# Attention of a hybrid encoder trunk: TensorE's order written out, products as a stream of steps between its parts, the sample keys in buffers of their own, the longest scores in a product's banks

## The chip, the cores and the metric

The kernel runs on one core of one Trainium2 chip. The core has a matrix engine (TensorE, PE in the profile, with its weight loads as PEld), a vector engine (VectorE, DVE), a scalar engine (ScalarE, ACT), a general engine (GpSimd, POOL) and SyncE (SP), which here issues transfers. Each engine works through its own queue of instructions in order; semaphores order the engines among each other. The metric is the device time of one execution in microseconds, the median of several runs; the profile comes from one execution, and its times have their zero at the start of that execution's span.

## The reference

The model is a trunk of two layers for 512 frames of one new stream (the prompt) and 8 running streams with 16 new frames each (the samples), 640 tokens in all, with 1024 features. What it computes, cut to what matters here:

```python
x += 0.5 * swiglu(rmsnorm(x, g1), w_gu1, w_down1)
h  = rmsnorm(x, gm)
z  = h @ w_in          # columns: conv B | conv C | conv V | q | k | v | gates
y_conv = B * causal_conv3(C * V)
# prompt: a frame reads its own chunk of 64 and the 8 before, 8 heads of 64
s = q @ k.T * 64 ** -0.5 + rel_bias[clipped distance]
y_attn = softmax(where(valid, s, -1e30)) @ v
# sample: 16 queries against 256 cached keys and their own 16
m = sigmoid(g_conv) * (y_conv @ w_conv_out) + sigmoid(g_attn) * (y_attn @ w_attn_out)
x += m @ w_o
x += 0.5 * swiglu(rmsnorm(x, g2), w_gu2, w_down2)
```

A final norm follows the layers. Outputs are the normed frames, the new keys and values, and the last two inputs of each convolution.

## The kernel before

The 640 tokens lie along the free axis, the features along the 128 partitions. All large products work in fp32 split in two parts: a weight tile of 128 × 128 is held as `whi` and `wlo`, an activation as `hhi` and `hlo` (with a suffix m for the mixer's norm), and a product sums hi·hi, hi·lo and lo·hi. `product` (L307 to L318) does this for one output tile: 8 weight tiles, three parts each, two halves of 320 tokens, 48 matmuls of 128x320 on L317. Its output `ps` is a tile of `acc`, PSUM's pool of two buffers with two banks each. The other PSUM pool, `att`, has four buffers with one bank each. Weights come in slabs of 512 KB: SP loads `raw` (L188), ACT rounds it to `whi` (L248), DVE takes the difference `wlo` (L253); there are three buffers of each.

A layer is a feed-forward part, the mixer and a second feed-forward part. The mixer norms x: `sums` (L400) adds the squares over the features with ten one-column matmuls (`npsm`), `roots` takes the root on ACT (L404) and the reciprocal on DVE (L405), `turn` (L410) spreads the result over a diagonal tile on DVE, and `nbcm` (L382) broadcasts it with matmuls into PSUM, from where ACT copies it to `rrm` (L383). The products do not wait for it: they take the unscaled x, and each result is scaled with `rrm` (`rr` in the code) on its way out of PSUM. The function `stats` that issues sums, root, turn and broadcast is called from within the first product of q, ahead of its sixth weight tile.

`attention` (L984) is the stage that the change touches. It projects q and k for each of the 4 pairs of heads (`qproj`, `kproj`: `pq`, `pk`), and v for all of them (`pv`, L1027). For each pair, `scores` issues for each block i of 128 queries the two heads' scores against the (i + 1) · 128 keys that a query of that block can see (`pss`, L1060; four blocks of 128 to 512 keys), and DVE adds the bias and takes the maximum while it reads them (L1062) into the tile `s`. `softmax` (L1188 to L1194) takes the exponent on ACT and normalises on DVE. `values` turns the weights (`ptp`, transposes on L1082, copied out by ACT and DVE on L1084), multiplies with v (`py`, L1095) and copies the result into `yas` (L1097). The samples follow: `sscores(b)` loads the cached keys and values of sample b (`kc` on L1126, `vc` on L1129, 512 KB each, and `vn` on L1132), copies the new keys behind the cached ones on POOL (L1133), computes the scores of all 8 heads (`spss`, L1136) and their softmax; `svalues(b)` transposes (`sptp`, L1151), copies out (`spt` on ACT, `spn` on DVE), multiplies with the values (`spy`, L1162), scales on ACT (`yx`, L1164) and transposes into the layout of `yas` (`ptx`, L1167).

`kc` and `vc` use the buffers of tag "s", two of them, which the prompt's weights `s` use as well. A new tile of that tag waits until the tile before the last has been read.

Beside the attention there are products that do not depend on it: the four channels of the convolution (`conv`: products `pc`, `pcv` and `pb`, each followed by DVE's work on the channel) and the first two gates (`pgate`). They are in the generator `others`, and each call of `other()` issues the next whole product. In `attention` no order is written out by hand: the scheduler of the compiler places each instruction in its engine's queue by its own estimate of when the operands are ready, so the code gives the data and a rough order only. The stage behind it (`outputs`) and the last product of the mixer have their order written (`manual_schedule`).

Of the kernel before, what the change touches and what calls it, by code (L numbers as in the profile page):

```python
# [138 lines left out]
def trunk(ctx: ExitStack, tc: tile.TileContext, xin, wst, small, pbias, samplebias, kcache, vcache,  # L139
# [167 lines left out]
    def product(ps, ops, at=()):  # L307
# [3 lines left out]
        for k, (xh, xl) in enumerate(ops):  # L311
# [3 lines left out]
            for j, (w, x) in enumerate(((wh, xh), (wh, xl), (wl, xh))):  # L315
                for a in range(2):
                    PE.matmul(ps[:, a, :HT], w, x[:, a * HT : (a + 1) * HT],  # L317
                              start=k == 0 and j == 0, stop=k == n - 1 and j == 2)  # L318

# [478 lines left out]
    def mixer(l, after):  # L798
        with tc.tile_pool(name=f"yp{l}", bufs=1, reuse_waits="tile") as yp:
# [5 lines left out]
            with tc.tile_pool(name=f"mp{l}", bufs=2, reuse_waits="tile") as mp:  # L805
# [3 lines left out]
                def gate(m, then=None):  # L809
                    pg = acc(f"pgate{l}_{m}")  # L810
                    product(pg, h)
# [10 lines left out]
                def others():  # L822
# [3 lines left out]
                    for m in range(2):  # L826
                        gate(m)
                        yield

                other = others()  # L830
                attention(l, h, st, stats, mp, yas, lambda: next(other, None))
# [152 lines left out]
    def attention(l, h, norms, stats, mp, yas, other):  # L984
# [11 lines left out]
        def qproj(p):  # L996
            pq = acc(f"pq{l}_{p}")
            product(pq, h, {5: stats} if p == 0 else {})
# [3 lines left out]
            for e in range(2):  # L1002
                r = slice(e * HD, (e + 1) * HD)
                POOL.tensor_copy(bd[r, :, p, e * TS : (e + 1) * TS],
                                 t[r, SEQ:].rearrange("p (b t) -> p b t", b=NB))

        def kproj(p):
            pk = acc(f"pk{l}_{p}")
            product(pk, h)
# [3 lines left out]
            POOL.tensor_copy(ks[:, p, :], t[:, SEQ:])  # L1013

        qproj(0)
        kproj(0)

# [26 lines left out]
        def scores(p):  # L1044
# [10 lines left out]
            for i in range(NQ):  # L1055
                w = (i + 1) * P
                pss = [att(f"pss{l}_{hh}_{i}")[:, :w] for hh in heads]
# [14 lines left out]
        def values(p):  # L1072
# [13 lines left out]
            for j in range(NQ):  # L1086
                for e in range(2):
                    turn(j, e)
                if j == 0:
# [9 lines left out]

        for p in range(npair):  # L1100
            scores(p)
            last = p == npair - 1
            if last:
                other()
                other()
            else:
                qproj(p + 1)
            vals = values(p)
            next(vals)
            if last:  # L1110
                other()
            else:
                kproj(p + 1)
# [8 lines left out]
        def sscores(b):  # L1122
            n = f"{l}_{b}"
            kc = mp.tile([P, offs[-1] + SEQ], F32, name=f"kc{n}", tag="s")
            kc = kc[:, : npair * KS].rearrange("p (a k) -> p a k", a=npair)
# [20 lines left out]
        def svalues(b):  # L1146
# [9 lines left out]
            DVE.tensor_copy(pn, ptp[:TS, 2 * P : 3 * P])  # L1156

# [6 lines left out]
            ACT.activation(yx, pys, AF.Copy, scale=st[:, 3, 0:1])  # L1164
            if b % G == 0:
# [10 lines left out]
        sscores(0)  # L1176
        for b in range(NB):
            if b + 1 < NB:
                sscores(b + 1)
            for _ in range(2 if b < 2 else 1):  # L1180
                other()
            svalues(b)
        other()
# [294 lines left out]
```

## Time and profile before

| | us |
|---|---|
| median of 3 runs | 2635.67 |
| lowest and highest | 2634.62, 2636.07 |
| the profiled execution | 2634.21 |
| its span in the profile | 2632.4 |
| TensorE busy | 2605.3 |
| DVE busy | 1832.0 |
| ACT busy | 1051.4 |
| POOL busy | 58.4 |

The span is what the profiler saw from the first to the last instruction; the execution's own time is 1.8 us longer. In rows of a timeline the first number is the start in microseconds from the span's start, the second the duration; then engine, line, operation, output and inputs by their names, shapes, and how often in a row; brackets at the end show the idle time of the engine before it and what released it. Matmuls overlap in a pipeline, so the pace is read from start to start and not from durations. In the view of waits a row has the total, the number of times and the longest in microseconds.

### The profile page before, as it was taken

To read this page: it belongs to the slowest core of one execution; us is meant where nothing else is said; L and a number is where in the kernel's file an instruction comes from. 1 tells how busy PE (TensorE), PEld (TensorE's weight loads), DVE (VectorE), ACT (ScalarE), POOL (GpSimd) and SP (SyncE) were. 2 spreads that over 40 slices of the span, in tenths; PEclk is the share of its full clock that TensorE was granted. 3 is DMA by queue.
4 is the path that set the end of the run, shared out by engine and by line. 5 is a ranking of instruction groups with operands and counts; after the bars stand their busy time and mean duration, and the time that the engine had idled before them with its cause. 6 is when DMAs were issued, how large, how long until landed. Compare 5 with 4: busy or idle time off the path is not lost.

```text
span 2632.4 us, 42588 instructions
## 1 busy us (share of the span) xinstructions
PE 2605.3 (99%) x17864; PEld 2544.0 (97%) x17864; DVE 1832.0 (70%) x2771; ACT 1051.4 (40%) x1586; POOL 58.4 (2%) x137
## 2 busy tenths in 40 slices
PE   8999999999999999999999999999999999999998
PEld 8999999888999999999999999998889999999998
DVE  7687676453677887767787677655546779867676
ACT  5343334332444543334453333334324445433333
POOL 0000000110000000000000000001010000000000
PEclk9999999999999999999999999999999999999999
DMA  3222222224122132222222222233241222222222
GB/s 130 77 100 81 79 91 99 104 97 140 69 93 81 65 106 88 73 89 81 81 81 96 88 82 73 89 103 112 96 146 57 89 81 73 97 89 81 80 92 78
DMA packets 73809, 237.07 MB, mean 90 GB/s; under 512 B 7984, under 2 KB 18864, under 8 KB 73616
## 3 DMA queue, kind: packets, MB, share of 16 engines
q1 hardware_dynamic: 70016, 223.90, 24.7%
q0 software_dynamic: 2880, 9.79, 1.0%
q8 instruction: 140, 2.29, 0.3%
q10 hardware_dynamic: 720, 0.65, 0.1%
q14 instruction: 53, 0.43, 0.1%
HBM read 225.85 MB, written 7.94 MB: 89 GB/s over the span
## 4 chain that ended last, share of the span: by engine, by line
PE 92%; DVE 4%; DMA 3%; ACT 1%; issue 1%; SPq 0%; DVEq 0%; ACTq 0%; POOLq 0%
PE pab L326 11%; PE pda L317 11%; PE pdb L317 11%; PE paa L326 10%; PE pcb L326 6%; PE pca L326 5%; PE py L317 4%; PE po L317 4%; PE qa L326 3%; PE pbb L326 3%; PE pba L326 3%; DMA kc<-in_kcache 2%; PE pq L317 2%; PE pgate L317 2%; PE pk L317 2%; PE pv L1027 2%
## 5 line engine op out<-in xcount | busy, mean ns | idle before, releaser
L253 DVE TENSOR_TENSOR wlo<-raw,whi 128x1024 fp32r<-128x1024 f32 (+2 forms) x492 | 530.7, 1083 | 162.5 <-ACT whi L248 162.4
L248 ACT CAST whi<-raw 128x1024 fp32r<-128x1024 f32 (+2 forms) x492 | 461.5, 941 | 395.3 <-PE pca L326 79.4
L326 PE MATMUL pab<-xhib,whi 128*128 128x320 f32 x704 | 218.4, 310 | 0.4 <-ACT u_b L721 0.4
L326 PE MATMUL pab<-xlob,whi 128*128 128x320 f32 x704 | 217.4, 309 | 0.0
L326 PE MATMUL pab<-xhib,wlo 128*128 128x320 f32 x704 | 217.4, 309 | 0.0
L326 PE MATMUL paa<-xhia,whi 128*128 128x320 f32 x640 | 198.2, 310 | 0.7 <-ACT c_a L657 0.5
L326 PE MATMUL paa<-xloa,whi 128*128 128x320 f32 x640 | 197.7, 309 | 0.0
L326 PE MATMUL paa<-xhia,wlo 128*128 128x320 f32 x640 | 197.7, 309 | 0.0
L317 PE MATMUL pda<-ahia,whi 128*128 128x320 f32 x704 | 160.4, 309 | 0.6 <-DVE x L787 0.6
L317 PE MATMUL pda<-aloa,whi 128*128 128x320 f32 x704 | 160.4, 309 | 0.0
L317 PE MATMUL pda<-ahia,wlo 128*128 128x320 f32 x704 | 160.4, 309 | 0.0
L317 PE MATMUL pdb<-alob,whi 128*128 128x320 f32 x656 | 149.6, 309 | 0.0
L317 PE MATMUL pdb<-ahib,whi 128*128 128x320 f32 x656 | 149.5, 309 | 0.0
L317 PE MATMUL pdb<-ahib,wlo 128*128 128x320 f32 x656 | 149.4, 309 | 0.0
L326 PEld LDWEIGHTS pab<-xhib,whi 128*128 128x128 f32 x704 | 132.2, 188 | 1.2 <-ACT u_b L721 0.9
L326 PEld LDWEIGHTS pab<-xlob,whi 128*128 128x128 f32 x704 | 132.2, 188 | 0.2
L326 PEld LDWEIGHTS pab<-xhib,wlo 128*128 128x128 f32 x704 | 132.2, 188 | 0.0
L326 PEld LDWEIGHTS paa<-xhia,whi 128*128 128x128 f32 x640 | 120.2, 188 | 1.3 <-ACT c_a L657 0.8
L326 PEld LDWEIGHTS paa<-xloa,whi 128*128 128x128 f32 x640 | 120.2, 188 | 0.1
L326 PEld LDWEIGHTS paa<-xhia,wlo 128*128 128x128 f32 x640 | 120.2, 188 | 0.0
L248 ACT CAST whi<-s 128x1024 fp32r<-128x1024 f32 (+1 forms) x96 | 94.2, 981 | 63.5 <-DVE s L192 52.0
L317 PEld LDWEIGHTS pda<-ahia,whi 128*128 128x128 f32 x704 | 117.6, 188 | 1.1 <-issue 1.1
(486 smaller groups left out, 6731.6 us busy)
## 6 DMA issues: line engine op xcount, KB each, us to landing
raw<-in_wst SPq DMA_DIRECT2D x384, 512.0 KB, 3.5
kc<-in_kcache SPq DMA_DIRECT2D x16, 512.0 KB, 4.3
vc<-in_vcache SPq DMA_DIRECT2D x16, 512.0 KB, 3.4
bias<-in_pbias POOLq DMA_DIRECT2D x16, 256.0 KB, 3.5
x<-in_xin SPq DMA_DIRECT2D x8, 320.0 KB, 5.4
out_ko<-k POOLq DMA_DIRECT2D x8, 320.0 KB, 2.4
out_vo<-v POOLq DMA_DIRECT2D x10, 256.0 KB, 3.0
out_yout<-x SPq DMA_DIRECT2D x8, 192.0 KB, 1.9
```

Source lines behind the costliest of these rows:

```text
L248: ACT.copy(hi[:, d], src[:, c])
L253: DVE.tensor_tensor(out=lo, in0=src, in1=hi.bitcast(F32), op=ALU.subtract)
L317: PE.matmul(ps[:, a, :HT], w, x[:, a * HT : (a + 1) * HT], start=k == 0 and j == 0, stop=k == n - 1 and j == 2)
L326: PE.matmul(ps, a, b, start=start and kp == 0 and j == 0, stop=stop and kp == NP - 1 and j == 2, skip_group_check=True)
L1027: PE.matmul(pv[t], xx[:, t * P : (t + 1) * P], w[:, kk * AW : (kk + 1) * AW], start=c == 0 and kk == 0 and j == 0, stop=c == KT // 2 - 1 a ...
```

## The change

`product` becomes the generator `steps`, which hands control back after each weight tile (6 matmuls); `product` itself runs it to the end. The products of q, k, the convolution and the gates are chained into one stream (`work`), and `fill(n)` issues the next n weight tiles of it. TensorE's order in `attention` is now the order in which the code issues: the stage stands under `manual_schedule` for that engine alone, the other engines keep the scheduler.

The order as written, in weight tiles: q_0 (with the norm's sums and broadcast, one directly behind the other, ahead of the sixth tile), k_0, v, 4 tiles; then for each pair the scores, 12 tiles, transposes of two key blocks, 2 tiles, transposes of the other two, 2 tiles, the weighted values. Then the scores of samples 0 and 1; for each sample 7 tiles (8 for odd ones), transposes, 2 tiles, values, the scores of the sample after the next, 2 tiles, the last transpose; at the end what is left of the stream.

The longest scores of the two heads of a pair (i = 3, 512 keys each) go to the two banks of one `acc` tile and are issued second. `kc` has its own tag, with two buffers.

```diff
--- before.py
+++ after.py
@@ -304,7 +304,7 @@
 
     tiles = Tiles()
 
-    def product(ps, ops, at=()):
+    def steps(ps, ops, at=()):
 
 
         n = len(ops)
@@ -316,6 +316,12 @@
                 for a in range(2):
                     PE.matmul(ps[:, a, :HT], w, x[:, a * HT : (a + 1) * HT],
                               start=k == 0 and j == 0, stop=k == n - 1 and j == 2)
+            if k < n - 1:
+                yield
+
+    def product(ps, ops, at=()):
+        for _ in steps(ps, ops, at):
+            pass
 
     def block(ps, s, half, ops, ks, start, stop):
 
@@ -807,8 +813,12 @@
                 gates = {}
 
                 def gate(m, then=None):
+                    for _ in gate_steps(m, then):
+                        pass
+
+                def gate_steps(m, then=None):
                     pg = acc(f"pgate{l}_{m}")
-                    product(pg, h)
+                    yield from steps(pg, h)
                     if then:
                         then()
                     gates[m] = tmp(f"g{l}_{m}")
@@ -824,11 +834,11 @@
                         yield from conv(l, c, h, rr, cn, ycs[c])
                     POOL.dma_start(co[l], cn)
                     for m in range(2):
-                        gate(m)
+                        yield from gate_steps(m)
                         yield
 
-                other = others()
-                attention(l, h, st, stats, mp, yas, lambda: next(other, None))
+                with tc.manual_schedule(engines={mybir.EngineType.PE}):
+                    attention(l, h, st, stats, mp, yas, others())
             with tc.tile_pool(name=f"gp{l}", bufs=1, reuse_waits="tile") as gp, \
                  tc.manual_schedule(engines=ORDERED):
                 hold[0] = True
@@ -981,7 +991,9 @@
         give(range(6, KT))
         return mo
 
-    def attention(l, h, norms, stats, mp, yas, other):
+    def attention(l, h, norms, stats, mp, yas, others):
+
+
         rr = norms.rr
         npair = H // 2
         nt = T // P
@@ -995,7 +1007,7 @@
 
         def qproj(p):
             pq = acc(f"pq{l}_{p}")
-            product(pq, h, {5: stats} if p == 0 else {})
+            yield from steps(pq, h, {5: stats} if p == 0 else {})
             t = qa[p] = mp.tile([P, T], F32, name=f"q{l}_{p}", tag="q")
             DVE.scalar_tensor_tensor(out=halves(t), in0=two(pq), scalar=HD ** -0.5,
                                      in1=halves(rr), op0=ALU.mult, op1=ALU.mult)
@@ -1003,17 +1015,32 @@
                 r = slice(e * HD, (e + 1) * HD)
                 POOL.tensor_copy(bd[r, :, p, e * TS : (e + 1) * TS],
                                  t[r, SEQ:].rearrange("p (b t) -> p b t", b=NB))
+            yield
 
         def kproj(p):
             pk = acc(f"pk{l}_{p}")
-            product(pk, h)
+            yield from steps(pk, h)
             t = ka[p] = mp.tile([P, T], F32, name=f"k{l}_{p}", tag="k")
             scaled(t, pk, rr)
             POOL.dma_start(ko[l, :, p, :], t)
             POOL.tensor_copy(ks[:, p, :], t[:, SEQ:])
-
-        qproj(0)
-        kproj(0)
+            yield
+
+        def work():
+            for p in range(1, npair):
+                yield from qproj(p)
+                yield from kproj(p)
+            yield from others
+
+        def fill(n):
+            for _ in range(n):
+                next(stream, None)
+
+        for _ in qproj(0):
+            pass
+        for _ in kproj(0):
+            pass
+        stream = work()
 
         rc = norms.r
         pv2 = [acc(f"pv{l}_{i}") for i in range(2)]
@@ -1052,9 +1079,14 @@
                 POOL.memset(bias[-1][0:CHUNK, SEQ - CHUNK :], NEG)
                 ss.append(mp.tile([P, offs[-1] + SEQ], F32, name=f"s{n}", tag="s"))
                 st.append(mp.tile([P, 4, NQ], F32, name=f"st{n}", tag="st"))
-            for i in range(NQ):
+
+            for i in (0, NQ - 1, *range(1, NQ - 1)):
                 w = (i + 1) * P
-                pss = [att(f"pss{l}_{hh}_{i}")[:, :w] for hh in heads]
+                if i == NQ - 1:
+                    both = acc(f"pss{l}_{p}")
+                    pss = [both[:, e, :w] for e in range(2)]
+                else:
+                    pss = [att(f"pss{l}_{hh}_{i}")[:, :w] for hh in heads]
                 for e in range(2):
                     r = slice(e * HD, (e + 1) * HD)
                     PE.matmul(pss[e], qa[p][r, i * P : (i + 1) * P], ka[p][r, :w], start=True, stop=True)
@@ -1086,7 +1118,7 @@
             for j in range(NQ):
                 for e in range(2):
                     turn(j, e)
-                if j == 0:
+                if j % 2:
                     yield
             py = att(f"py{l}_{p}")
             for j in range(NQ):
@@ -1097,20 +1129,15 @@
             ACT.copy(yas[:, p, 0:SEQ], py)
             yield
 
+        fill(4)
         for p in range(npair):
             scores(p)
-            last = p == npair - 1
-            if last:
-                other()
-                other()
-            else:
-                qproj(p + 1)
+            fill(12)
             vals = values(p)
             next(vals)
-            if last:
-                other()
-            else:
-                kproj(p + 1)
+            fill(2)
+            next(vals)
+            fill(2)
             next(vals)
 
 
@@ -1121,8 +1148,8 @@
 
         def sscores(b):
             n = f"{l}_{b}"
-            kc = mp.tile([P, offs[-1] + SEQ], F32, name=f"kc{n}", tag="s")
-            kc = kc[:, : npair * KS].rearrange("p (a k) -> p a k", a=npair)
+            kc = mp.tile([P, npair * KS], F32, name=f"kc{n}", tag="kc")
+            kc = kc.rearrange("p (a k) -> p a k", a=npair)
             SP.dma_start(kc[:, :, :PAST], kcache[l, b])
             vraw = mp.tile([P, offs[-1] + SEQ], F32, name=f"vc{n}", tag="s")
             vraw = vraw[:, : 2 * AW].rearrange("p (a k) -> p a k", a=2)
@@ -1154,6 +1181,7 @@
             pn = mp.tile([TS, P], F32, name=f"spn{n}", tag="spn")
             ACT.copy(pt, ptp[:, : 2 * P].rearrange("p (a b) -> p a b", a=2))
             DVE.tensor_copy(pn, ptp[:TS, 2 * P : 3 * P])
+            yield
 
             pys = att(f"spy{n}")[:, :P]
             for j, (w, v) in enumerate(((pn, vn), (pt[:, 0], vraw[:, 0]), (pt[:, 1], vraw[:, 1]))):
@@ -1162,6 +1190,7 @@
                     PE.matmul(pys[r], w[:, r], v[:, p * P : (p + 1) * P], start=j == 0, stop=j == 2)
             yx = mp.tile([P, P], F32, name=f"yx{n}", tag="yx")
             ACT.activation(yx, pys, AF.Copy, scale=st[:, 3, 0:1])
+            yield
             if b % G == 0:
                 ptx[0] = att(f"ptx{n}")
             PE.transpose(ptx[0][:, (b % G) * P : (b % G + 1) * P], yx, ident)
@@ -1174,13 +1203,18 @@
                         ptx[0][r].rearrange("p (b a e t) -> p a b e t", b=G, a=npair, e=2)[:, :, :, e, :])
 
         sscores(0)
+        sscores(1)
         for b in range(NB):
-            if b + 1 < NB:
-                sscores(b + 1)
-            for _ in range(2 if b < 2 else 1):
-                other()
-            svalues(b)
-        other()
+            vals = svalues(b)
+            fill(7 + b % 2)
+            next(vals)
+            fill(2)
+            next(vals)
+            if b + 2 < NB:
+                sscores(b + 2)
+            fill(2)
+            next(vals, None)
+        fill(KT * KT)
 
     def softmax(s, st, parts, whole=True):
 
@@ -1197,12 +1231,12 @@
     def conv(l, c, h, rr, cn, y):
         n = f"{l}_{c}"
         pc = acc(f"pc{n}")
-        product(pc, h)
+        yield from steps(pc, h)
         ct = tmp(f"ct{n}")
         scaled(ct, pc, rr)
         yield
         pv = acc(f"pcv{n}")
-        product(pv, h)
+        yield from steps(pv, h)
         vt = tmp(f"vt{n}")
         scaled(vt, pv, rr)
         u = tp.tile([P, UW], F32, name=f"u{n}", tag="t")
@@ -1225,7 +1259,7 @@
                                      in1=samp(y), op0=ALU.mult, op1=ALU.add)
         yield
         pb = acc(f"pb{n}")
-        product(pb, h)
+        yield from steps(pb, h)
         bt = tmp(f"bt{n}")
         scaled(bt, pb, rr)
         DVE.tensor_tensor(out=y, in0=y, in1=bt, op=ALU.mult)
```

## The prediction

> **What bounds the kernel now.** I read the page first: busy times, the granted clock, the chain that ended last.
>
> ```profile
> span 2632.4 us, 42588 instructions
> PE 2605.3 (99%) x17864; PEld 2544.0 (97%) x17864; DVE 1832.0 (70%) x2771; ACT 1051.4 (40%) x1586; POOL 58.4 (2%) x137
> PE 92%; DVE 4%; DMA 3%; ACT 1%; issue 1%; SPq 0%; DVEq 0%; ACTq 0%; POOLq 0%
> ```
>
> TensorE is busy for 99% of the span, and it makes 92% of the chain that ended last. An edit that does not change the number of products can therefore gain only TensorE's idle time and the time in which it is called busy but does not advance at its pace. The idle time of the whole span is 2632.4 − 2605.3 = 27.1 us. The change touches one stage in each layer, the attention; in layer 0 that is 447 to 690 us, in layer 1 1746 to 1987 us. I cut that stretch into windows of 20 us (columns: time, sum, then busy time of PE, PEld, DVE, ACT, POOL, clock, DMA share, GB/s).
>
> ```profile
> 580.00:600.00 20.00, 19.03 (x137) 16.05 (x136) 7.27 (x16) 4.89 (x10) 0.88 (x4) 1.00 0.45 150
> 700.00:720.00 20.00, 19.98 (x136) 19.71 (x135) 18.38 (x27) 7.52 (x12) 0.00 (x0) 1.00 0.07 27
> ```
>
> The clock is full (1.00). The idle time of the stage begins in the window from 580 (19.03 busy of 20), where the samples begin and where DVE and ACT have more than half their time free. Then the view of waits says what TensorE waits for there, and the page's list of transfers how long such a load takes.
>
> ```profile
> PE spss L1136 <- DMA kc<-in_kcache: 9.4, 14, 1.3
> kc<-in_kcache SPq DMA_DIRECT2D x16, 512.0 KB, 4.3
> ```
>
> It is the cached keys of a sample: 14 of 16 scores wait for them, 9.4 us in all, which is the largest wait of TensorE in the whole trace. A load takes 4.3 us to land, and its buffer comes free only when an older tile of tag "s" has been read.
>
> **The change part by part.** Counts of instructions stay the same on every engine; TensorE's order changes in the attention stage only, and DVE, ACT, POOL and SP follow it there.
>
> *Keys in buffers of their own.* The load of kc no longer waits for a value or score tile to be read; it waits for the scores of two samples before. In the written order 54 products stand between spss_0 and spss_2, the shortest such distance, so a load of 4.3 us has 54 × 0.147 = 7.9 us of cover (the pace of 0.147 is in the rows below), 3.6 more than it takes. Loads 0 and 1 need no free "s" tile at all and leave in the pairs' stage. Behind kc on SP's queue stand vc, vn and the weights (raw); kc moves ahead of these by some microseconds, and none of them has a buffer free sooner. Gain: the 9.4 us. If the cover were gone, a load would be late by what is missing, up to 4.3 us at a sample. I take 9.4, the row's; the bounds are 9.4 and 5, should half of the waits return.
>
> *Prompt scores.* The rows show a block of weighted values (py), the block of scores behind it (pss), the product behind that, and DVE's last read of a score.
>
> ```profile
> 510.91 2.38 PE L1095 MATMUL py<-pt,v 128*64 128x512 f32 x16
> 513.21 3.12 PE L1060 MATMUL pss<-k,q 64*128 64x128 f32 x16
> 516.27 0.56 PE L317 MATMUL pq<-hlom,whi 128*128 128x320 f32 x2
> 516.90 0.69 DVE L1062 CUSTOM_DVE_ANT_0 s<-pss,bias 128x512 f32<-128x512 f32 x1
> ```
>
> From start to start, pss takes 516.27 − 513.21 = 3.06 us; py, which moves the same 1280 columns for two heads side by side, takes 513.21 − 510.91 = 2.30 us. The excess is the wait for the four one-bank score buffers, which DVE empties. Now the two longest scores lie in a two-bank product tile and are issued second, so that only the last two scores reuse a bank, and by columns that is (128 + 512 + 256)/1280 × 2.30 = 1.6 us after the block began. If pss then runs like py, the eight blocks give 8 × 0.76 = 6.1 us; the other bound is 0, if DVE is in other work at that moment. I take 6.0, the py row's. The price: the product tile is held until DVE has read it, and pk needs it 24 products later, 2.3 + 24 × 0.147 = 5.8 us after the block's start. DVE's last read ends at 516.90 + 0.69 = 517.59, 4.4 us after it. That hides it by 1.4 us; past that each microsecond would cost 8, one for each pair.
>
> *Fewer changes between kinds of work.* The next rows show the transposes (ptp) of the last pair with single products between them, ahead of them two pairs of products at their own pace.
>
> ```profile
> 577.73 0.46 PE L317 MATMUL pb<-hhim,whi 128*128 128x320 f32 x2
> 578.02 0.46 PE L317 MATMUL pb<-hlom,whi 128*128 128x320 f32 x2
> ...
> 582.13 1.25 PE L1082 MATMUL ptp<-ident,s 128*128 128x128 f32 x10
> 583.14 0.39 PE L317 MATMUL pc<-hhim,whi 128*128 128x320 f32 x1
> 583.52 0.33 PE L1082 MATMUL ptp<-ident,s 128*128 128x128 f32 x1
> ...
> 584.03 2.37 PE L1095 MATMUL py<-pt,v 128*64 128x512 f32 x16
> 586.34 0.56 PE L317 MATMUL pc<-hlom,whi 128*128 128x320 f32 x2
> 586.74 0.46 PE L317 MATMUL pc<-hhim,wlo 128*128 128x320 f32 x2
> 587.99 0.67 PE L1136 MATMUL spss<-kc,bd 128*32 128x272 f32 x8 [0.37 <-DMA kc<-in_kcache]
> 672.96 0.64 PE L1162 MATMUL spy<-vc,spt 128*32 128x128 f32 x16
> ```
>
> Two products take 578.02 − 577.73 = 0.29 us, 0.147 each. The first two behind py take 586.74 − 586.34 = 0.40, that is 0.10 more; the product ahead of spss or ptp pays about as much (583.14 to 583.52 with one transpose of 0.1 is 0.09 over). A change there and back costs some 0.2 us. In program order before, such blocks of other work stand alone 120 times; after, 88 times. Sixteen of these 32 are the single transposes: 582.13 → 584.03 is 1.90 us, and 12 × 0.10 + 2 × 0.147 + 0.10 = 1.6, so 0.3 × 8 = 2.4 us, with 16 × 0.2 = 3.2 as the other bound. The other sixteen are the samples' scores, which now follow spy or py directly. Bounds 0 and 16 × 0.2 = 3.2; I take 1.5, the middle, as no row shows spss behind spy. The Trainium skill, page "TensorEngine Tiling (Array Packing)", section "Key Properties", says that a change of tiling mode drains TensorE; spss and the end of spy have one tile, 128*32 in the last two rows, so by it 14 of the 16 would be had in full, and the sum would stand 1.3 us lower.
>
> *The norm's sums.* This part goes against the change. Rows of TensorE and DVE round the sums npsm and the broadcast nbcm (the turn, L410, is the broadcast's operand):
>
> ```profile
> 452.21 1.20 PE L400 MATMUL npsm<-ones,ya 128*128 128x1 f32 x10
> 453.27 0.54 PE L317 MATMUL pq<-hhim,whi 128*128 128x320 f32 x2
> 451.27 0.82 DVE L370 TENSOR_TENSOR ya<-ya,sqm 128x640 f32<-128x640 f32 x1
> 454.04 0.82 DVE L410 TENSOR_TENSOR ya<-ident,ninvm 128x640 f32<-128x640 f32 x1
> ```
>
> Before, the scheduler put npsm behind 36 products of pq_0 and nbcm behind 19 more, and neither waits. As written, npsm comes after 30 products and nbcm directly behind it. TensorE reaches npsm 6 × 0.147 = 0.88 us earlier, at 451.33, and the sum that it reads is ready at 451.27 + 0.82 = 452.09: 0.8 us idle. npsm runs to 453.2; the root, the reciprocal and the turn end at 454.04 + 0.82 = 454.86: 1.65 us idle. Everything behind on TensorE, all of q, k and v, moves by these 2.4 us. Layer 1 has the same work: 4.8 us for both, bounds 4.4 (one change of kind is saved in each) and 5.
>
> *Samples' values.* A sample is now 7 or 8 weight tiles, transposes (sptp), two tiles (12 products), spy, spss of the sample after the next, two tiles, ptx. Twelve products are 1.76 us, and spy needs DVE's small copy spn. Where a convolution has just ended, DVE is behind:
>
> ```profile
> 669.08 0.46 PE L317 MATMUL pb<-hhim,wlo 128*128 128x320 f32 x2
> 669.58 0.82 DVE L415 TENSOR_TENSOR bt<-pb,rrm 128x640 f32<-128x640 f32 x1
> 670.40 1.23 DVE L253 TENSOR_TENSOR wlo<-raw,whi 128x1024 fp32r<-128x1024 f32 x1
> 671.54 0.82 DVE L1231 TENSOR_TENSOR yc<-yc,bt 128x640 f32<-128x640 f32 x1
> 672.28 0.27 DVE L1156 COPY spn<-sptp 16x128 f32<-16x128 f32 x1
> ```
>
> spn ends 672.55, 3.17 us after the products of pb_3 ended (669.38); the written order reaches spy_6 0.35 + 1.76 = 2.1 us after them. So 1.0 us at sample 6, and 0.2 at sample 4, where one weight tile stands between: 2.4 us for both layers. At the other samples the convolution's end lies at least 3.5 us ahead of spy, or behind it; nothing there, as long as DVE does nothing longer than a 1.23 us split plus the copy of 0.27. The range takes 0 to 5.
>
> *Softmax of the prompt*, at nothing. Scores begin at 513.21 and the second head's normalisation starts here:
>
> ```profile
> 521.81 1.28 DVE L1194 TENSOR_SCALAR s<-s,st 128x128 f32<-128x128 f32 x4
> ```
>
> It ends at 523.1, 9.9 us after the scores began; twelve tiles of products put the first transpose 2.3 + 72 × 0.147 = 12.9 us after them. The cover is 3 us; without it, each microsecond missing would cost 8 (once in each pair).
>
> **Sum.** −9.4 − 6.0 − 2.4 − 1.5 + 4.8 + 2.4 = −12.1 us. The profiled execution took 2634.21 us (its span and 1.8 us around it), 1.46 under the median of the runs, 2635.67. So 2622.1 for such an execution, and 2623.6 for the median.
>
> **Rivals.** *The gain is larger*: the merged blocks give their 3.2, ptp 3.2, pss 6.1 and the samples wait nothing: −9.4 − 6.1 − 3.2 − 3.2 + 4.4 = −17.5, 2618. For it: DVE is half idle in the stage. Against: the spn chain is in the rows.
>
> *The clock falls in the norm's wait.* The last rows of TensorE before the end and its first rows:
>
> ```profile
> 2623.71 0.61 PE L1303 MATMUL npsf<-ones,sqf 128*128 128x1 f32 x4 [0.69 <-ACT sqf L1296]
> 2625.34 0.92 PE L1318 MATMUL nbcf<-fsum,ones 128*128 128x256 f32 x2 [1.02 <-DVE fsum L410]
> 2624.00:2628.00 4.00, 1.24 (x5) 0.53 (x5) 3.97 (x11) 0.26 (x1) 0.00 (x0) 0.71 0.78 275
> ...
> 8.00 0.74 PE L317 MATMUL poa<-hhia,whi 128*128 128x320 f32 x2
> 8.54 0.74 PE L317 MATMUL poa<-hloa,whi 128*128 128x320 f32 x2
> ```
>
> At the end, after small sums and idle times of 0.69 and 1.02 us, the clock falls to 0.71 on average in the window from 2624; at the start, pairs of products take 8.54 − 8.00 = 0.54 us in place of 0.29. The new wait looks alike: 0.8 idle, 1.1 of one-column products, 1.65 idle, 3.5 us in all. With six slow pairs, as at the start, 6 × 0.25 = 1.5 us a layer, +3: 2626.6. Against it: neither idle stretch alone is longer than 1.7 us. The Trainium skill, page "TensorE: Matmul & The Clock Gate", Part 1, says that the clock goes to half after an idle window of about 3.4 us; by that rule this wait is just long enough if the sums count as idle, and the time would be this rival's.
>
> *No net change*: TensorE comes some 6 us earlier in each layer to the gates and outputs, where DVE is 18.38 of 20 us busy (the window from 700). Were DVE's queue as far behind as before, the 12 us would be given back there: 2635. Against it: in the attention stage DVE has ample time to come ahead as well.
>
> *Slower*: in the samples' stage the order is now fixed, and a late spn, spt or yx stops TensorE, with all products behind it. There are 16 samples. If DVE is typically behind by a scaling, a split and a second scaling (0.82 + 1.23 + 0.82, as above) whenever sptp comes, spy comes 0.82 + 1.23 + 0.82 + 0.27 − 1.76 = 1.4 us late, and ptx, whose operand passes through a queue as well, half of that: 16 × 2.1 = 34 us against the 14.5 saved without the term of 2.4: 2655. It decides from 0.9 us a sample. Against it: the window from 580 shows DVE at 7.27 of 20 us.
>
> *The change doesn't do what it says*: TensorE's order stays the scheduler's. The program order shows the opposite.
>
> **How the numbers follow.** Forecast 0.55 (2623.6, own range 2618 to 2630), larger gain 0.12, clock 0.15, no net change 0.09, slower 0.08, no effect 0.01. What a measurement tells from no change is about 0.2%, 5.3 us: faster is below 2630.4. The first three are faster: 0.82; no change and no effect 0.10; slower 0.08. The range of 8 in 10 goes from the larger gain, with a microsecond or two below it, to a forecast with all costs at their upper bounds, pss gaining half and no merging (−9.4 − 3 − 2.4 + 5 + 5 = −4.8, 2631) and a microsecond more: 2616 to 2632.
>
> **What would show it.** Right: the wait of spss for kc gone; eight pss blocks of 2.3 us; a new wait of TensorE for DVE at nbcm of some 1.6 us and at npsm of 0.8 in each layer; a wait at spy_6 of about 1 us; 88 blocks. Wrong: waits for DVE or ACT at most samples, a pss block still at 3 us, a wait for ptp, pk waiting for the scores' tile, or a clock under 1.00 right behind nbcm.

## The result

| | median us | lowest to highest | span of the profiled execution |
|---|---|---|---|
| before | 2635.14 (4 runs) | 2634.49 to 2636.07 | 2632.4 |
| changed | 2620.64 (4 runs) | 2620.43 to 2621.95 | 2618.7 |

The ratio is 0.9946, with a 95% interval of 0.9929 to 0.9963: 14.5 us faster, 13.7 by the spans. The forecast was 2623.6. It lies close, but two of its terms were far off, in opposite directions, and one of the two was off because what the clock rival describes happened as well.

The page of the changed kernel, with the same lines as before the change:

```profile
span 2618.7 us, 42583 instructions
PE 2594.6 (99%) x17864; PEld 2542.4 (97%) x17864; DVE 1831.0 (70%) x2771; ACT 1053.2 (40%) x1586; POOL 46.5 (2%) x137
PE 93%; DVE 5%; ACT 1%; issue 1%; DMA 0%; DVEq 0%; ACTq 0%
```

TensorE's busy time fell by 10.7 us with the same 17864 matmuls, so part of what counted as busy before the change was not work at the full pace; the idle time fell by 3.0 us only. DMA's 3% of the chain is gone, DVE's share rose by one point. The view of TensorE's waits (total, times, longest) says why:

```profile
PE nbcm L388 <- DVE ya L416: 3.0, 2, 1.5
PE spy L1190 <- DVE spn L1183: 1.9, 2, 0.9
PE npsm L406 <- DVE ya L376: 1.3, 2, 0.7
```

No row for kc is left. Three new rows stand for it, 6.2 us in all: the norm's broadcast and sums in each layer and spy_6. They are the waits that the prediction had listed. What it had put to a rival is in TensorE's timeline behind the sums (start, duration, instruction) and in two windows, one for each layer:

```profile
451.00 0.46 PE L317 MATMUL pq<-hhim,wlo 128*128 128x320 f32 x2
452.10 1.28 PE L406 MATMUL npsm<-ones,ya 128*128 128x1 f32 x10 [0.65 <-DVE ya L376]
454.89 2.21 PE L388 MATMUL nbcm<-ya,ones 128*128 128x320 f32 x4 [1.51 <-DVE ya L416]
456.43 1.20 PE L317 MATMUL pq<-hhim,whi 128*128 128x320 f32 x2
457.43 0.73 PE L317 MATMUL pq<-hlom,whi 128*128 128x320 f32 x2
457.97 0.73 PE L317 MATMUL pq<-hhim,wlo 128*128 128x320 f32 x2
458.50 0.52 PE L317 MATMUL pq<-hhim,whi 128*128 128x320 f32 x2
...
455.00:459.00 4.00, 4.00 (x13) 3.30 (x14) 0.00 (x0) 0.85 (x2) 0.00 (x0) 0.57 0.02 4
1748.00:1752.00 4.00, 3.93 (x13) 3.39 (x14) 0.02 (x1) 0.85 (x2) 0.00 (x0) 0.61 0.00 0
```

Behind the wait, pairs of products come every 0.54 us (457.43 to 457.97) in place of 0.29, and the granted clock is 0.57 and 0.61 of full speed on average over four microseconds. In the trace's record of the clock it is half from 455.21 to 458.63 and from 1748.87 to 1752.28, and full around that. In layer 0 the fall comes within the broadcast, in layer 1 near its end; the first products behind it run at half clock in both.

The prompt's scores stand between py and the stream as forecast:

```profile
517.03 2.38 PE L1127 MATMUL py<-pt,v 128*64 128x512 f32 x16
519.33 2.43 PE L1092 MATMUL pss<-k,q 64*128 64x128 f32 x16
521.69 0.56 PE L317 MATMUL pq<-hhim,whi 128*128 128x320 f32 x2
```

521.69 − 519.33 = 2.36 us, against 3.06 before.

To see where the 13.7 us come from, the stage is cut at five starts that the timelines show: first product of q, first of v, first prompt score, first sample score, and the last ptx. As the written order moves products from one part to another, only the first column and the total (q to the first matmul of qa, behind the gates) compare with before.

| layer | | q to v | v to pss | pss to spss | spss to last ptx | total |
|---|---|---|---|---|---|---|
| 0 | before | 16.31 | 27.32 | 97.44 | 94.09 | 267.83 |
| 0 | changed | 20.48 | 30.83 | 84.51 | 98.35 | 262.43 |
| 1 | before | 16.31 | 27.32 | 97.77 | 96.38 | 270.45 |
| 1 | changed | 20.44 | 30.84 | 84.50 | 98.35 | 262.38 |

The stage won 5.4 and 8.1 us, which is the whole difference but 0.2 us. Layer 0 won less because it had lost less to kc before (3.5 us of waits, 5.9 in layer 1). Both layers pay 4.1 to 4.2 us between q and v.

### The profile page after: what moved, and what is told of

Same layout as the page of the kernel before. It is cut to its first block, busy times and chain, and to the rows that moved or that the text cites. A ratio compares the mean times of both kernels' runs of the same rounds, so it can differ in the third digit from the quotient of the medians.

```text
span 2618.7 us, 42583 instructions
## 1 busy us (share of the span) xinstructions
PE 2594.6 (99%) x17864; PEld 2542.4 (97%) x17864; DVE 1831.0 (70%) x2771; ACT 1053.2 (40%) x1586; POOL 46.5 (2%) x137
## 4 chain that ended last, share of the span: by engine, by line
PE 93%; DVE 5%; ACT 1%; issue 1%; DMA 0%; DVEq 0%; ACTq 0%
PE pab L332 11%; PE pda L317 11%; PE pdb L317 11%; PE paa L332 11%; PE pcb L332 6%; PE pca L332 5%; PE py L317 4%; PE po L317 4%; PE qa L332 3%; PE pbb L332 3%; PE pba L332 3%; PE pcv L317 2%; PE pb L317 2%; PE pk L317 2%; PE pv L1054 2%; PE pgate L317 2%
```

## The experiments

keys_alone starts from the kernel before, values_gap from sums_late, turns_joined from values_gap, all others from the changed kernel. How long the clock stays down behind the norm differs from run to run, so the stretches of the profiles are read beside the medians. The diffs are cut to the lines that matter.

### The norm's sums

Three kernels move the sums and the broadcast. In sums_late, `stats` is cut in two (`stats[0]` the sums, root and turn, `stats[1]` the broadcast), the sums behind 36 products of q_0 and the broadcast behind all 48:

```diff
-            yield from steps(pq, h, {5: stats} if p == 0 else {})
+            yield from steps(pq, h, {6: stats[0]} if p == 0 else {})
+            if p == 0:
+                stats[1]()
```

> The changed kernel with the norm's sums behind 36 products of q_0 (as the scheduler had them) and the broadcast behind all 48, so that 12 products lie between. Theory: the two waits (0.65 and 1.51 us) and the fall of the clock behind them are the whole difference of 4.15 us a layer between the start of q and the start of v (20.48 after, 16.31 before); without the waits the clock stays at 1.00, that stretch takes 16.3 to 16.6 us, and the kernel about 8 us less than the changed one: span 2610.5, median about 2612.5. Rival: the clock falls for another reason (the one-column sums themselves, or the lag of DVE and ACT); then only the idle time of 2.2 us a layer goes, the stretch takes some 18.3 us and the span is about 2614.5.

Measured: median 2611.98 (2611.74 to 2612.31), ratio to before 0.9916 [0.9901, 0.9931], span 2610.3; q to v 16.30 and 16.31 us. TensorE in the same place:

```profile
451.75 1.20 PE L408 MATMUL npsm<-ones,ya 128*128 128x1 f32 x10
454.66 1.24 PE L390 MATMUL nbcm<-ya,ones 128*128 128x320 f32 x4
...
455.00:459.00 4.00, 4.00 (x27) 3.76 (x26) 1.96 (x2) 1.36 (x3) 0.57 (x2) 1.00 0.21 70
```

No wait, clock 1.00, and the stretch takes what it took before the change. The 8.4 us of span are the whole price of the place that the change gave the sums and the broadcast.

sums_part, with `stats` cut in two as well, keeps the sums where the change has them and puts one weight tile between them and the broadcast:

```diff
-            yield from steps(pq, h, {5: stats} if p == 0 else {})
+            yield from steps(pq, h, {5: stats[0], 6: stats[1]} if p == 0 else {})
```

> The changed kernel with one weight tile (6 products, 0.88 us) between the norm's sums and its broadcast, so that the idle time is 0.65 us ahead of the sums and about 0.5 ahead of the broadcast. Theory: the clock falls because some 3.4 us hold next to no work for TensorE; broken up by six products it stays at 1.00, and the stretch from q to v takes 17.5 us (3.0 less than in the changed kernel), span about 2612.7. Rival: any wait there lets the clock fall; then the gain is the 0.9 us of idle time alone, the stretch takes 19.5 us, span about 2617.

Measured: median 2617.36 (2616.53 to 2617.72), span 2615.8. The two layers differ. Layer 0 takes 17.98 us from q to v, layer 1 19.62, with the same waits (0.65 and 0.52; 0.66 and 0.52). The windows behind the broadcast, the first of layer 0, the second of layer 1:

```profile
455.00:459.00 4.00, 3.98 (x24) 3.67 (x25) 0.77 (x2) 1.90 (x3) 0.00 (x0) 1.00 0.01 4
1746.00:1750.00 4.00, 3.88 (x12) 3.09 (x13) 0.06 (x1) 0.85 (x2) 0.00 (x0) 0.57 0.00 0
```

So the theory held in one layer and the rival in the other. A wait that is broken up may or may not cost the clock; its idle time alone does not decide. Where it does, it costs 19.62 − 17.98 = 1.64 us, as the waits are the same.

sums_one_wait moves the sums one tile later and leaves the broadcast behind them, so that only the second wait is left:

```diff
-            yield from steps(pq, h, {5: stats} if p == 0 else {})
+            yield from steps(pq, h, {6: stats} if p == 0 else {})
```

> The changed kernel with the norm's sums one tile later (behind 36 products), the broadcast still directly behind them: no wait ahead of the sums, 1.5 us ahead of the broadcast, so a stretch of 2.6 us (sums of 1.1, idle 1.5) without full products in place of 3.3. Theory: the clock falls by the length of such a stretch, and 2.6 us is short of it: clock 1.00, q to v 17.8 us, span 2613.5. Rival: an idle time of 1.5 us behind one-column products is enough: q to v 19.5 to 20.5 us, span 2617 to 2619.

Measured: median 2618.51 (2617.47 to 2618.66), span 2616.8, q to v 19.49 and 19.55 us. Timeline and windows of layer 0:

```profile
451.67 1.20 PE L406 MATMUL npsm<-ones,ya 128*128 128x1 f32 x10
454.39 2.50 PE L388 MATMUL nbcm<-ya,ones 128*128 128x320 f32 x4 [1.51 <-DVE ya L416]
...
453.00:455.00 2.00, 0.61 (x1) 0.50 (x2) 1.01 (x2) 0.18 (x1) 0.00 (x0) 0.79 0.00 0
455.00:457.00 2.00, 2.00 (x6) 1.33 (x5) 0.00 (x0) 0.50 (x2) 0.00 (x0) 0.50 0.03 8
```

The theory fell: 454.39 − 451.67 = 2.7 us with only one-column products and 1.51 us of idle time were enough, in both layers, and the clock was already down in the window from 453, at the broadcast's start. Removing the first wait of 0.65 us won 0.9 to 1.0 us a layer, and no more.

The record of the clock in the traces shows what decides. Without a kernel's first 20 and last 11 us, each stretch at half clock lasts 3.41 us, or two or three times that, and within one execution all changes of the clock lie whole multiples of 3.413 us apart: the two falls of the changed kernel, 455.21 and 1748.87, are 379 of them apart. The clock thus changes only on a grid of 3.41 us. Its place differs from execution to execution, so the same wait can lie on it in different ways. In sums_part the clock falls at 1746.17; the point of the grid 379 steps earlier, in layer 0, is 452.52. These are the pieces of the grid round the waits, layer 0 first:

```profile
452.52:455.93 3.41, 2.89 (x19) 2.39 (x19) 1.01 (x2) 0.34 (x2) 0.00 (x0) 1.00 0.24 97
1742.76:1746.17 3.41, 2.31 (x17) 2.05 (x17) 1.53 (x3) 0.27 (x1) 0.00 (x0) 1.00 0.44 151
1746.17:1749.59 3.42, 3.42 (x9) 2.62 (x10) 0.00 (x0) 0.85 (x2) 0.00 (x0) 0.50 0.00 0
```

In layer 1 both waits lie in one piece, which holds ten one-column sums and 7 full matmuls (six products and one of the broadcast), and the clock falls behind it. In layer 0 the waits lie in two pieces, and the second one holds nine sums and 10 full matmuls (six products and the broadcast's four). Counted by columns (320 are one product), in all 14 traces together, each of the 31 falls comes behind a piece with the work of at most nine products, and no piece at full clock with ten or more is followed by one. No run moves the grid on purpose, but the count leaves no exception.

### The keys' buffers

keys_shared is the changed kernel with kc back in tag "s":

```diff
-            kc = mp.tile([P, npair * KS], F32, name=f"kc{n}", tag="kc")
-            kc = kc.rearrange("p (a k) -> p a k", a=npair)
+            kc = mp.tile([P, offs[-1] + SEQ], F32, name=f"kc{n}", tag="s")
+            kc = kc[:, : npair * KS].rearrange("p (a k) -> p a k", a=npair)
```

> The changed kernel with kc back in the two buffers of tag s; everything else, the written order too, as changed. Theory: the buffers of their own gave the 9.4 us of waits back, so spss waits for kc's load again, 14 times or more, and as spss stands earlier now (right behind spy of the sample before the last, whose values still hold a buffer) the waits are longer than before: at least 9 us, likely 20 to 50, span 2630 to 2670. Rival: the written order alone covers the loads; then the span stays within 2 us of 2618.7 and no wait for kc shows.

Measured: median 2718.1 (2717.29 to 2719.11), ratio 1.0319 [1.0303, 1.0334]. The row of waits, one sample in the timeline and a window of the stage:

```profile
PE spss L1163 <- DMA kc<-in_kcache: 63.8, 16, 4.6
...
607.81 1.14 PE L1163 MATMUL spss<-kc,bd 128*32 128x272 f32 x8 [4.26 <-DMA kc<-in_kcache]
608.88 0.90 PE L317 MATMUL pc<-hhim,whi 128*128 128x320 f32 x2
609.58 0.74 PE L317 MATMUL pc<-hlom,whi 128*128 128x320 f32 x2
610.11 0.74 PE L317 MATMUL pc<-hhim,wlo 128*128 128x320 f32 x2
...
600.00:620.00 20.00, 15.74 (x112) 14.18 (x111) 3.74 (x8) 2.40 (x5) 0.41 (x3) 0.83 0.33 107
```

All 16 scores wait, about a landing each. 97.4 us of span are lost against 63.8 us of waits: behind the waits pairs of products come 0.53 us apart (609.58 to 610.11) for a while, and the clock of the window is 0.83. The expected range (20 to 50) had left the clock out. The written order needs the buffers.

keys_alone does the converse: the kernel before with the two lines of the change for kc (those of the diff above, the other way round) and nothing else.

> The kernel before with kc in two buffers of its own and nothing else changed, TensorE's order in the hands of the scheduler. Theory: the waits for kc (9.4 us) are a matter of the buffers, so they go: span 2632.4 - 9.4 to - 10.6 = 2622 to 2623, median near 2625.5. Rival: the scheduler places spss by its own estimate of when the load lands, and moves it forward with the earlier load, so that waits of some size stay: 3 to 9 us are left, span 2625 to 2632.

Measured: median 2625.65 (2625.25 to 2626.16), ratio 0.9969 [0.9957, 0.9982], span 2623.7. The row for kc is gone. 8.7 us are won, 8.0 of them in the two stages, somewhat under the theory's 9.4 to 10.6. A likely reason, which no run tests: the scheduler moved the scores forward, directly behind spy, and set a transpose among them. One sample of it, with the row of ACT that makes the transpose's operand:

```profile
619.85 0.64 PE L1162 MATMUL spy<-vc,spt 128*32 128x128 f32 x16
620.31 0.62 PE L1136 MATMUL spss<-kc,bd 128*32 128x272 f32 x2
620.99 0.33 PE L1167 MATMUL ptx<-ident,yx 128*128 128x128 f32 x1
621.24 0.66 PE L1136 MATMUL spss<-kc,bd 128*32 128x272 f32 x6
620.56 0.37 ACT L1164 ACTIVATE yx<-spy,sst 128x128 f32<-128x128 f32 x1 [2.31 <-PE spy L1162]
```

From the scores' start to ptx it is 620.99 − 620.31 = 0.68 us, with two of their matmuls in it: ptx stands in TensorE's queue ahead of the other six, and its operand yx ends at 620.93. This is an order by estimate, with a wait of its own.

The buffers alone bring 8.7 of the 13.7 us. The written order and the banks bring the other 5, which is a gain of over 13 less the 8.4 that the norm's broadcast costs.

### The prompt's scores

banks_four takes both halves of the edit back (order 0, 1, 2, 3, all in the one-bank buffers), banks_order keeps the order alone, banks_acc the product tile alone:

```diff
# banks_four
-            for i in (0, NQ - 1, *range(1, NQ - 1)):
+            for i in range(NQ):
...
-                if i == NQ - 1:
+                if False:
# banks_order
-                if i == NQ - 1:
+                if False:
# banks_acc
-            for i in (0, NQ - 1, *range(1, NQ - 1)):
+            for i in range(NQ):
```

> The changed kernel with the prompt's scores as before the change: four blocks in the order 0, 1, 2, 3, all in the four one-bank buffers. Theory: the blocks then wait for DVE's reads as before, 3.06 us in place of 2.36 (3.25 for the first of a layer), so eight blocks cost 6.3 us more: span 2618.7 + 6.3 = 2625.0. Rival: the blocks ran long for the scheduler's order of DVE (a weight split between the reads); then part of it stays saved, blocks of 2.4 to 2.8 us, span 2619.5 to 2622.5.

> The changed kernel with the prompt's scores in the order 0, 3, 1, 2, but all in the four one-bank buffers. Theory: the wait comes from the number of banks, so the order alone does not help: the two longest scores stay in a bank for their 0.69 us reads, and blocks take about 3 us or more, some 6 us over the changed kernel for the eight. Rival: the order does it (no bank is taken again until a short block has been read); then blocks of 2.4 to 2.6 us, at most 2 us over it. Read from the blocks and the stage, as the clock behind the norm's broadcast differs from run to run by about a microsecond.

> The changed kernel with the longest scores in the product tile but in the order 0, 1, 2, 3. Theory: banks decide, order hardly: block 2 now takes its banks 0.7 us after the start, when DVE has read one of the first two scores at best, so it waits some 0.5 us: blocks of 2.6 to 2.9 us, 2 to 4 us over the changed kernel for all eight. Rival: order does not matter at all, blocks of 2.36 us.

Medians 2626.22, 2631.47 and 2626.64. The second block of layer 0 with the product behind it, in banks_four, banks_order and banks_acc:

```profile
520.41 3.12 PE L1092 MATMUL pss<-k,q 64*128 64x128 f32 x16
523.46 0.56 PE L317 MATMUL pq<-hhim,whi 128*128 128x320 f32 x2
...
520.67 3.66 PE L1092 MATMUL pss<-k,q 64*128 64x128 f32 x16
524.26 0.56 PE L317 MATMUL pq<-hhim,whi 128*128 128x320 f32 x2
...
520.48 3.03 PE L1092 MATMUL pss<-k,q 64*128 64x128 f32 x16
523.43 0.56 PE L317 MATMUL pq<-hhim,whi 128*128 128x320 f32 x2
```

That is 3.05, 3.59 and 2.95 us, against 2.36 with both. The stretch from the first prompt score to the first sample score, four blocks, grows from 84.5 us to 87.5 and 87.2 in banks_four, so 5.7 us in both layers belong to the edit. The order alone makes the blocks longer than before, the banks alone win 0.1; only the two together win 0.7 a block. Both single halves came out worse than expected: in the same stretch banks_order is 9.9 us over the changed kernel in both layers (expected some 6), and banks_acc 4.9 (expected 2 to 4). No row here shows which read each block waits for, so why the order matters this much stays open.

### Blocks of other work

scores_apart sets the samples' scores one weight tile behind spy:

```diff
+            fill(1)
             if b + 2 < NB:
                 sscores(b + 2)
-            fill(2)
+            fill(1)
```

> The changed kernel with the samples' scores one weight tile behind spy in place of directly behind it, so 12 blocks of other work (6 samples in 2 layers) stand alone again; products between spy and ptx stay 12. Theory: a block that stands alone costs the change of kind there and back, 0.2 us by the rows: 12 x 0.2 = 2.4 us more, span 2621.1. Rival: spy and spss side by side paid the change anyway; then the span stays within 0.5 us of 2618.7.

Measured: from the first sample score to the last ptx 100.29 us in both layers against 98.35, so 3.9 us for 12 blocks, 0.32 each (median 2625.08, 2620.97 to 2625.48; the span, 2623.7, holds another microsecond between q and v). TensorE round one sample:

```profile
606.64 0.65 PE L1190 MATMUL spy<-vc,spt 128*32 128x128 f32 x16
607.22 0.56 PE L317 MATMUL pb<-hhim,whi 128*128 128x320 f32 x2
607.62 0.45 PE L317 MATMUL pb<-hlom,whi 128*128 128x320 f32 x2
607.91 0.45 PE L317 MATMUL pb<-hhim,wlo 128*128 128x320 f32 x2
608.29 0.67 PE L1163 MATMUL spss<-kc,bd 128*32 128x272 f32 x8
608.89 0.56 PE L317 MATMUL pb<-hhim,whi 128*128 128x320 f32 x2
```

In the changed kernel spss follows the start of those 16 matmuls of spy by 0.46 us (605.14 to 605.60); here the next product follows it by 607.22 − 606.64 = 0.58. So leaving spy costs 0.12, the first pair 0.40 in place of 0.29, the way back to spss 0.09 (607.91 to 608.29 is 0.38). These three make the 0.32.

turns_apart cuts the prompt's transposes into three groups with products between them, in place of two:

```diff
-                if j % 2:
-                    yield
+                yield
...
-            next(vals)
-            fill(2)
-            next(vals)
-            fill(2)
+            for n in (1, 1, 0, 2):
+                next(vals)
+                fill(n)
             next(vals)
```

> The changed kernel with the prompt's transposes in three groups in place of two (products between the first and the second group), 8 more blocks that stand alone. Theory: each costs 0.2 to 0.32 us like the samples' scores: the stretch from the first prompt score to the first sample score is 0.8 to 1.3 us longer in each layer (84.5 in the changed kernel). Rival: transposes are full tiles like the products, so a change to them and back costs less, 0 to 0.4 us a layer.

Measured: 85.11 us in both layers, from the first prompt score to the first sample score, against 84.51 and 84.50; that is 0.15 us for each of the four blocks of a layer, between the two expectations (the median, 2620.61, is the changed kernel's). A group of transposes costs half of what a group of the samples' scores does.

### The samples' values, and a faster kernel

values_gap starts from sums_late and gives DVE's copy at sample 6 one weight tile more:

```diff
-            fill(7 + b % 2)
+            fill(7 + b % 2 - (b == 6))
             next(vals)
-            fill(2)
+            fill(2 + (b == 6))
```

> The kernel of sums_late with sample 6 taking 6 weight tiles ahead of its transposes and 3 behind them (7 and 2 before), so that 18 products cover DVE's copy spn. Theory: the wait of 0.94 us at spy_6 in each layer goes and nothing takes its place: span 2610.3 - 1.9 = 2608.4. Rival: the transposes come earlier by 0.9 us, DVE takes the work in another order or the wait moves to another operand (spt, yx, the scaled pb); then 0 to 1 us is gained, span 2609.3 to 2610.5.

Measured: median 2610.45 (2610.22 to 2610.73), ratio to before 0.9910 [0.9895, 0.9925], span 2608.7, 1.6 us under sums_late; the samples' stretch fell from 98.36 and 98.35 to 97.33 and 97.34 us, and no row of spy is left among the waits. turns_joined starts from there and sets each ptx directly ahead of the next sptp:

```diff
-            fill(7 + b % 2 - (b == 6))
+            fill((9 if b else 7) + b % 2 - (b == 6))
+            next(was, None)
             next(vals)
...
-            fill(2)
-            next(vals, None)
+            was = vals
```

> The kernel of values_gap with each sample's last transpose ptx put directly ahead of the next sample's transposes sptp, so 14 of 16 blocks of ptx no longer stand alone. Theory: each saves the change of kind, 0.2 us: 2.8 us less than values_gap, span 2605.6. Rival: ptx is a single matmul whose change of kind overlaps with the products around it (0.03 us to the next product in the rows); then at most 0.5 us is gained, span 2608.

Measured: median 2610.61 (2610.22 to 2610.81), span 2608.7, nothing won. The samples' stretch is 0.24 us longer, for this is back among the waits:

```profile
PE spy L1194 <- DVE spn L1187: 0.6, 2, 0.3
```

Without these 0.3 us a layer, 14 blocks fewer gave at most 0.1 us, so a single ptx between products costs next to nothing, and the rival was right. values_gap is the fastest kernel here: 10.2 us under the changed one by the medians.

## Why the prediction was right, and where it was not

The direction was right and most of the mechanism too, but that the total came within 3 us of the forecast is luck: two errors of 3.5 to 3.7 us met. Term by term:

*Keys* (forecast −9.4): right. The row is gone, and two runs show that the buffers, not the order, remove it: in keys_shared TensorE's wait came back for all 16, in keys_alone it is gone without the order.

*Prompt scores* (−6.0): right. Eight blocks of 2.36 us; banks_four puts the edit at 5.7 us. The reason was told as banks that DVE holds too long. The runs show that this is not enough: the banks alone win next to nothing, the order alone loses.

*Single transposes* (−2.4): near. 16 blocks at 0.15 us, as turns_apart measures a group, are 2.4. But a lone ptx cost nothing, so that price need not hold for single ones. Counted in both timelines as time beyond 0.147 us a product, the transposes of a pair went from 2.49 to 2.20 us (from 2.59 in the first pair), and py, which now stands apart from them, costs 0.09 more: 1.8 us in both layers.

*Merged scores* (−1.5, bound −3.2): wrong, the step that mis-sized a term. I priced a change at 0.2 us from products round py and a transpose and took half, for want of a row with spss behind spy. scores_apart measures 0.32 a block behind spy; if the four scores behind py gain as much, 16 of them are 5.2 us, past the bound of 3.2. The Trainium skill, page "TensorEngine Tiling (Array Packing)", section "Key Properties", pointed the right way: by it nothing drains between spy and spss, and the gain is had in full. It doesn't explain the whole price, as transposes have the products' own 128*128 tile and still cost 0.15.

*The norm's sums* (+4.8): the waits came where the text put them, 0.65 and 1.51 us for 0.8 and 1.65. But the stretch lost 4.17 and 4.13 us, 8.3 in all, and sums_late gives 8.4 back. The step that failed was to leave the clock to a rival with a chance of 0.15; a clock under 1.00 right behind nbcm, one of the prediction's own signs of being wrong, is there in both layers. That rival's price, 1.5 us a layer from the rows at the kernel's start, was nearly right; measured it is 1.64 between the layers of sums_part, and 2.0 as what is left of 4.15 less 2.16 of idle time. My reason against it, that neither idle time alone is longer than 1.7 us, was no reason: in sums_one_wait 1.51 us behind one-column products was enough. The Trainium skill, page "TensorE: Matmul & The Clock Gate", Part 1, names an idle window of about 3.4 us that runs freely. The traces agree with the length, 3.41 us, and with the free run; but the window need not be idle, as the clock also fell behind 2.7 us of sums and idle time, and behind a window with seven full matmuls.

*Samples' values* (+2.4): 1.9 by the view of waits, 2.0 by values_gap. At sample 6 it is 0.94 us where 1.0 was worked out. The wait of 0.2 at sample 4 did not come: the row has two waits, one a layer.

*Softmax, product tile* (nothing): no row of waits for ptp, pk or the prompt's scores, as forecast.

With the sizes from the experiments: −9.4 − 5.7 − 2.4 − 5.2 + 8.3 + 1.9 = −12.5, against −13.5 in the stage. Counted block by block in the two timelines, as for the transposes, the prompt's scores give 6.3, the transposes 1.8 and the samples' blocks without their waits 6.0, and the sum is −13.3. So most of the missing microsecond lies in the samples' blocks; whether it belongs to the merged scores or to the start behind the old waits is not settled.

Of the rivals, "no net change" and "slower" fell: DVE's queue cost TensorE nothing in the samples' stage outside sample 6, and the gates behind took nothing back (the total won is what the stage won).

## What to carry to other kernels

Where an order is written by hand, a chain of small steps on other engines (sums, root, reciprocal, broadcast) needs products between its ends, as many as the chain is long; here 18 products a layer, moved from behind the broadcast to ahead of it (six ahead of the sums, twelve behind them), were worth over 8 us in two layers, more than the 4.3 us of idle time that they fill, because a quiet TensorE loses its clock as well. Count the groups of unlike matmuls in program order and price each kind by itself: here scores of 32 columns cost 0.32 us a group, full transposes 0.15, a lone ptx none. When two halves of an edit go together (which bank, in what order), try each alone: one can be worth nothing, or less, without the other.

## What the runs showed of the hardware

In these traces the clock falls to half and rises again only on a grid of 3.41 us, whose place differs from one execution to the next. It fell behind pieces of the grid with the work of at most nine products of 0.147 us, and behind none with ten or more (31 falls in 14 traces). Sums of one column hardly count: 2.7 us of sums and idle time were enough (sums_one_wait). One piece at half clock costs about 1.6 us (sums_part). In layer 0 of scores_apart it was two, 454.06 to 460.89, and q to v took 21.64 us there.

A kernel that sits at this edge scatters: scores_apart ran three times at 2624.79 to 2625.48 us with a granted clock of 0.997 and once at 2620.97 with 0.999, while sums_late and values_gap, without a fall, stayed within 0.6 us. The clock is not the only cause of scatter: the kernel before ran from 2632.14 to 2636.83 us, always at 0.998 or 0.999.

A wait can cost half as much again as its length: 63.8 us of waits for keys made a kernel 97.4 us longer, most of the rest being products at half clock behind the waits.
